# A two-pass prompt attention: the turning of the log-sums put later, the first pass started further ahead, the first loads reordered

## The chip, the core and the metric

The kernel runs on one core of one Trainium2 chip. The metric is device time in microseconds of one execution. The kernel is one decoding step of a small decoder (one convolution layer, then one attention layer) for a prompt of 1024 tokens and for eight samples of one token each.

## What is computed

The change lies in the attention of the prompt. Cut to that, the reference is:

```python
# q, k, v: (1024 tokens, 16 heads, 64); C = cumsum of the log forget gates, per head
def fox_attend(q, k, v, C):              # swept in blocks of 128 queries
    s = einsum('bqhd,bkhd->bhqk', q, k) / sqrt(64)
    s = s + C[query] - C[key]
    s = where(key <= query, s, -inf)
    p = softmax(s, axis=-1)
    return einsum('bhqk,bkhd->bqhd', p, v)
# layer output: x + (o * silu(z)) @ w_out
```

Ahead of it stand a gated convolution layer and the projections to q, k, v and z, behind it the output projection. All of these, and the attention of the eight samples over their paged caches, are untouched by the change.

## The kernel before

The program runs through stages: the convolution layer, the projections (with the samples' attention worked in beside them), the prompt attention, and the output projection. In the profiled execution the prompt attention begins at about 980 us and ends at about 1312 us of a span of 1442.5 us.

**Two passes.** Products are made to nearly full precision from a high and a low part of each operand, so a product takes two or three matmuls. The attention of a head is done in two passes over the scores.

- The *first pass*, `first(h, ...)`, goes through the eight query blocks of 128 in the order `QORD` = 0, 4, 1, 5, 2, 6, 3, 7. For block i, TensorE writes the scores against (i+1)*128 keys to PSUM (L1162, L1163, and L1165 for the mask), VectorE takes the negative maximum (`nm`, L1166), and ScalarE takes exp with that bias and sums it (L1168). Below, F5.7 is block 7 of head 5; a head's first pass is eight such items.
- After blocks 3 and 7, `logsum` (L1178 to L1182) makes for four blocks at once the maximum plus the logarithm of the sum: one small ScalarE instruction, then three small VectorE instructions of 128x4 elements. Its inner function `turn` (L1186 to L1190) lets TensorE transpose the result (`lt`), ScalarE copy it out of PSUM, and SyncE send it by two small DMAs to two rows of the head's query tile `q2`. Below, T5.0 and T5.1 are the two turns of head 5.
- The *second pass*, `second(h, ...)`, makes the scores again, transposed (`st`, L1225, L1226), with the rows that `turn` wrote standing in the product, so that exp gives the softmax itself. It goes through two halves c of 512 queries and, in each, pairs of key blocks: six items a head. Below, S5.12 is head 5, half 1, key blocks 2 and 3. ScalarE takes the exp to `pt` (L1235), GpSimd (POOL in the profile) rounds it to `ph` (L198), GpSimd or VectorE takes the rest `pl` (L1239), and TensorE weighs the values with both (`weigh`, L1205, L1206, into `po`). At a half's end ScalarE copies one part out (`tb`, L1209) and VectorE adds (`og`, L1210); after an odd head VectorE and ScalarE gate and split the pair of heads (L1252, `oh` L1254, `ol` L1255).

**PSUM.** The large score tiles of both passes (F of blocks 4 to 7, S items 00, 10, 12 and 14) share one pool of two buffers (`psS`); the small ones and the turns share one of three (`psQ`); the weighed values have a single buffer (`psO`). So a large item starts when the exp of the one two before it in that pool is done, and the weighing of a half starts when `og` of the half before is done.

**What sets the order.** `firsts()` and `seconds()` yield an item at a time. `LEAD` first-pass items are written out ahead, then the two are taken in turn by the pattern `PAT` = FSFSFSFFSFSFFS, eight F and six S to a head. Steps that should come later are put off by `put_off(n, f)`, which runs f once more than n items have gone by: exp by `DEXP` = 1, `logsum` by `DEXP + DLS` = 1 item, `turn` by `DLT` items after its `logsum`. What is written out in this order is then ordered once more when the program is built: a scheduler lists each engine's instructions by the order written and by its own estimate of when each can start. Every engine then runs its list strictly in order.

**Loads.** A head's tiles are fetched by `load_qk(h)` (eight DMAs, six of them of 256 KB) and `load_rest(h)` (the values `vh` of 512 KB, and `sz` of 512 KB for each pair of heads), all issued by SyncE, which also issues the small DMAs of `turn`. A DMA there waits until the one eight before it has landed. Heads 0 and 1 are loaded before the stage; head 2's tiles and head 0's values are the stage's first loads. From then on `seconds()` loads values one head and query and key tiles three heads ahead of the second pass.

Of the kernel before, what the change touches and what calls it, by code (L numbers as in the profile page):

```python
# [99 lines left out]
ST = 2  # L100
FT = 1
VE = 2
LEAD = 13
W0E = 2
THR = 2
CHQ = 1
# [12 lines left out]
START = "w0 n0 t0 w1 n1 n2"  # L119
X0V = 1  # L120
DLS = 0
DLT = 3
PAT = "FSFSFSFFSFSFFS"


def f32(ap):
    return ap.bitcast(F32)
# [7 lines left out]
def tile_step(ctx, tc, xt, st, stT, vecs, cwT, win, wout, wqkv, wf, wbo, hvec, qgf, ck, cv, cf, pt,  # L135
# [16 lines left out]
    def table(name):  # L152
        tc.keep_in_program_order(S.preload_act_table_set(name))
# [478 lines left out]
    def load_qk(h):  # L632
        pool = hd if h % 4 > 1 else h0
        q1, q2, k1, k2 = [pool.tile([P, 1024], F32R, tag=nm, name=nm, bufs=2) for nm in ("q1", "q2", "k1", "k2")]
        fs = slice(h * HD, (h + 1) * HD)

        for out, src in ((q1[0:HD], qt_scr[0, fs]), (k1[0:HD], kt_scr[0, fs]), (q1[HD:P], qt_scr[1, fs]), (k1[HD:P], kt_scr[0, fs]),
                         (q2[0:HD], qt_scr[0, fs]), (k2[0:HD], kt_scr[1, fs]), (q2[HD:HD + 4], c_scr[h, 0:4]), (k2[HD:HD + 6], c_scr[h, 4:10])):
            SY.dma_start(out=f32(out), in_=src)
        return q1, q2, k1, k2  # L640

    def load_rest(h):
        vh = hd.tile([P, 8, P], F32R, tag="vh", name="vh", bufs=VHB)
        SY.dma_start(out=f32(vh), in_=vt_scr[h].rearrange("(i p) f -> p i f", p=P))
        hp, e = divmod(h, 2)
        if e == 0:
            sz = szs[hp] = ld.tile([P, T], F32, tag="sz", name="sz", bufs=1)
            SY.dma_start(out=sz, in_=z_scr[hp])
        return vh

    qk0 = []
# [470 lines left out]
    with pat:  # L1122
# [8 lines left out]
        def qbank(name):  # L1131
            if OBANK:
                return psO.tile([P, 512], F32, tag="o", name=name)
            return psQ.tile([P, 512], F32, tag="q", name=name)
# [7 lines left out]
        def put_off(n, f):  # L1142
            off_.append([n, f])

        def catch_up(n=1):
            for x in list(off_):
                x[0] -= n
                if x[0] < 0:
                    off_.remove(x)
                    x[1]()  # L1150

        def first(h, q1, q2, k1, k2):
            nm = sm.tile([P, 8], F32, tag="nm", name="nm")
            sr = sm.tile([P, 8], F32, tag="sr", name="sr")
            for qi in QORD:
                nk = (qi + 1) * P
                qsl = slice(qi * P, (qi + 1) * P)
                ss = qbank("ss") if nk in SMF else psS.tile([P, 1024], F32, tag="s", name="ss")
                for b0 in range(0, nk, 512):
                    w = min(512, nk - b0)  # L1160
                    lastb = b0 + w == nk
                    PE.matmul(ss[:, b0:b0 + w], q1[:, qsl], k1[:, b0:b0 + w], start=True, stop=False)  # L1162
                    PE.matmul(ss[:, b0:b0 + w], q2[0:HD + 4, qsl], k2[0:HD + 4, b0:b0 + w], start=False, stop=not lastb)  # L1163
                    if lastb:
                        PE.matmul(ss[:, qsl], identb, maskb, start=False, stop=True)  # L1165
                V.tensor_reduce(out=nm[:, qi:qi + 1], in_=ss[:, :nk], axis=AX.X, op=ALU.max, negate=True)  # L1166
                def expsum(ss=ss, nk=nk, qi=qi):
                    S.activation(out=ss[:, :nk], in_=ss[:, :nk], func=AF.Exp, bias=nm[:, qi:qi + 1], accum_out=sr[:, qi:qi + 1])  # L1168

                put_off(DEXP, expsum)  # L1170
                catch_up()
                if qi % 4 == 3:
                    put_off(DEXP + DLS, lambda qi=qi: logsum(h, qi // 4, nm, sr, q2))
                yield nk

        def logsum(h, c, nm, sr, q2):
            cs = slice(c * 4, c * 4 + 4)
            S.activation(out=sr[:, cs], in_=sr[:, cs], func=AF.Ln)  # L1178
            V.tensor_tensor(out=nm[:, cs], in0=nm[:, cs], in1=sr[:, cs], op=ALU.subtract)
            lc = sm.tile([P, 8], F32R, tag="lc", name="lc")  # L1180
            V.tensor_copy(out=lc[:, 0:4], in_=nm[:, cs])
            V.tensor_tensor(out=lc[:, 4:8], in0=nm[:, cs], in1=f32(lc[:, 0:4]), op=ALU.subtract)  # L1182

            def turn():
                ps = qbank("lt")
                PE.transpose(f32r(ps[0:8, 0:P]), lc, identr)  # L1186
                lt = sm.tile([8, P], F32, tag="lt", name="lt")
                S.copy(out=lt, in_=ps[0:8, 0:P])
                for a in range(2):
                    SY.dma_start(out=f32(q2[HD + 4 + a:HD + 5 + a, c * 512:(c + 1) * 512]).rearrange("a (t q) -> a t q", t=4), in_=lt[4 * a:4 * a + 4])  # L1190

            put_off(DLT, turn)

# [60 lines left out]
                    S.copy(out=oa.hi(hp, a, b - a), in_=og[:, a:b])  # L1254
                    V.tensor_tensor(out=oa.lo(hp, a, b - a), in0=og[:, a:b], in1=f32(oa.hi(hp, a, b - a)), op=ALU.subtract)  # L1255

        hs = qk0 + [load_qk(2)]
        vhs = [load_rest(0)]
        table("natural_log_exp_and_others")
        oa = Act("o")  # L1260

        def firsts():
            for h in range(NH):
                yield from first(h, *hs[h])

        def seconds():
            for h in range(NH):
                if h + 1 < NH:
                    vhs.append(load_rest(h + 1))
                if h + 3 < NH:  # L1270
                    hs.append(load_qk(h + 3))
                yield from second(h, *hs[h], vhs[h])


        if MAN:
            pat.enter_context(tc.manual_schedule(engines={getattr(mybir.EngineType, e) for e in MAN.split()}))
        fs_, ss_, n = firsts(), seconds(), 0
        for _ in range(LEAD):
            next(fs_)
        while True:  # L1280
            x = next(fs_, None) if PAT[n % len(PAT)] == "F" else None
# [6 lines left out]
    with ExitStack() as po_:  # L1288
# [16 lines left out]
        def resid(hf, t0, tn):  # L1305
            x = wk.tile([P, 512], F32, tag="xr", name="xr", bufs=10)
            SY.dma_start(out=x[:tn], in_=x1_scr[t0:t0 + tn, hf * 512:(hf + 1) * 512])
            return x
# [44 lines left out]
        for t in range(8):  # L1353
# [7 lines left out]
            x = resid(1, t * P, P)  # L1361
# [56 lines left out]
```

## Time and profile before

| | us |
|---|---|
| median of 3 runs (lowest, highest) | 1446.85 (1446.19, 1448.22) |
| the profiled execution, its own time | 1444.18 |
| its span, first to last instruction | 1442.5 |
| prompt attention within the span | about 980 to 1312 |
| TensorE busy over the span | 1266.6 (88%) |
| VectorE busy over the span | 1151.2 (80%) |
| GpSimd busy over the span | 800.8 (56%) |
| ScalarE busy over the span | 732.2 (51%) |

The shares are means over stages with different limits; the change touches only the attention stage, so that stage is read by itself: by stretches, by the waits in it, and instruction by instruction in one pair of heads (the pattern of work repeats every two heads, since which engine makes `pl` differs between even and odd heads). In the rows, PE is TensorE, PEld its weight loads, DVE VectorE, ACT ScalarE, POOL GpSimd and SP SyncE. A wait in brackets behind an instruction is the time its engine stood idle before it and what released it.

### The profile page before, as it was taken

What the parts mean: (1) busy time and instruction counts of PE and PEld (TensorE: products, weight loads), DVE (VectorE), ACT (ScalarE), POOL (GpSimd) and SP (SyncE); (2) the same over time, 40 slices, a digit from 0 to 9 for tenths busy, and PEclk for the clock granted to TensorE, in tenths of its full rate; (3) what the DMA queues carried; (4) which work ended last, traced back from release to release, by engine and by line L of the source; (5) the groups of instructions that cost most, each with busy time, mean ns of one, the idle gap of its engine ahead of it and who ended that gap; (6) DMA issues with size and microseconds to landing.
All of it is one profiled execution on the core that took longest, in us unless ns stands there. A gap on an engine that the chain in (4) does not pass through costs nothing. (4 is left out here: it accounts for less than half of the span.)

```text
span 1442.5 us, 21436 instructions
## 1 busy us (share of the span) xinstructions
PE 1266.6 (88%) x6543; PEld 1050.8 (73%) x6543; DVE 1151.2 (80%) x1844; ACT 732.2 (51%) x1922; POOL 800.8 (56%) x603
## 2 busy tenths in 40 slices
PE   5999999988999799987997979796988888885988
PEld 4999999987778587765776768695766666664866
DVE  6999999998844489999899989873688787876851
ACT  6666554755745666765662223114666665662100
POOL 4598895982220063447466555750666565666940
PEclk9999999998999899999998989898899998998989
DMA  5111010111244666788788888888455555413841
GB/s 209 57 59 59 31 30 20 45 44 62 81 146 125 177 184 209 232 229 260 242 266 274 275 269 267 248 210 186 106 123 122 114 134 120 90 45 109 280 159 38
DMA packets 155531, 213.95 MB, mean 148 GB/s; under 512 B 14058, under 2 KB 82282, under 8 KB 155400
## 3 DMA queue, kind: packets, MB, share of 16 engines
q1 hardware_dynamic: 137879, 202.09, 48.1%
q10 hardware_dynamic: 16896, 8.39, 2.0%
q0 software_dynamic: 640, 2.10, 0.5%
q8 instruction: 52, 0.85, 0.3%
q14 instruction: 64, 0.52, 0.1%
HBM read 165.22 MB, written 48.13 MB: 148 GB/s over the span
## 5 line engine op out<-in xcount | busy, mean ns | idle before, releaser
L347 POOL TENSOR_TENSOR cvt<-cvt 128x512 f32<-128x512 f32 (+4 forms) x179 | 242.0, 1388 | 44.5 <-ACT cvt L343 41.7
L906 POOL TENSOR_TENSOR kh<-kh,qb 128x512 f32<-128x512 f32 x96 | 137.4, 1446 | 131.4 <-DMA kh<-in_ck 87.9
L352 DVE SCALAR_TENSOR_TENSOR acc<-u,cw,acc 128x512 f32<-128x512 f32 (+4 forms) x285 | 195.8, 742 | 0.1
L198 POOL TENSOR_SCALAR ph<-pt 128x896 fp32r<-128x896 f32 (+1 forms) x96 | 90.7, 960 | 153.3 <-ACT pt L1235 139.7
L685 POOL TENSOR_TENSOR av<-av,vt 128x512 f32<-128x512 f32 x80 | 134.2, 1698 | 71.0 <-DVE vt L683 64.2
L1105 PE MATMUL pq<-wp,acth 128*128 128x512 f32 x384 | 158.4, 412 | 0.0
L1107 PE MATMUL pq<-wp,actl 128*128 128x512 f32 x384 | 155.2, 404 | 0.0
L1106 PE MATMUL pq<-wp,acth 128*128 128x512 f32 x384 | 154.8, 403 | 0.0
L1166 DVE TENSOR_REDUCE nm<-ss 128x1 f32<-128x128 f32 (+7 forms) x128 | 93.3, 750 | 75.5 <-PE ss L1165 62.7
L683 DVE TENSOR_TENSOR vt<-vt,lg 128x512 f32<-128x512 f32 x112 | 127.8, 1173 | 13.4 <-DMA vt<-in_cv 13.2
L343 ACT ACTIVATE cvt<-u,cw 128x512 f32<-128x512 f32 (+4 forms) x195 | 125.7, 717 | 16.2 <-DVE wl L271 8.3
L1168 ACT ACTIVATE ss<-ss,nm 128x128 f32<-128x128 f32 (+7 forms) x128 | 91.1, 712 | 68.6 <-DVE nm L1166 68.3
L1239 POOL TENSOR_TENSOR pl<-pt,ph 128x384 fp32r<-128x384 f32 (+2 forms) x56 | 103.5, 1854 | 2.3
L1162 PE MATMUL ss<-k,q 128*128 128x512 f32 (+2 forms) x192 | 78.9, 411 | 13.6 <-ACT ss L1168 12.6
L1235 ACT ACTIVATE pt<-st 128x896 f32<-128x896 f32 (+1 forms) x96 | 75.5, 805 | 30.1 <-PE st L1233 19.4
L1107 PEld LDWEIGHTS pq<-wp,actl 128*128 128x128 f32 x384 | 74.3, 193 | 18.7 <-issue 0.8
L1105 PEld LDWEIGHTS pq<-wp,acth 128*128 128x128 f32 x384 | 74.7, 195 | 17.8 <-ACT hsq L826 1.0
L1106 PEld LDWEIGHTS pq<-wp,acth 128*128 128x128 f32 x384 | 74.7, 194 | 16.7 <-issue 0.5
L907 DVE TENSOR_REDUCE lg<-kh 128x8 f32<-128x512 f32 x128 | 82.7, 673 | 4.6 <-POOL kh L906 4.5
L1205 PE MATMUL po<-ph,vh 128*128 128x512 f32 x192 | 72.4, 382 | 7.8 <-DVE og L1210 4.5
L1226 PE MATMUL st<-q,k 70*128 70x512 f32 (+1 forms) x192 | 67.1, 367 | 9.8 <-DMA q<-lt 9.8
L1225 PE MATMUL st<-q,k 128*128 128x512 f32 (+1 forms) x192 | 72.4, 384 | 2.3 <-ACT pt L1235 2.1
(337 smaller groups left out, 3777.5 us busy)
## 6 DMA issues: line engine op xcount, KB each, us to landing
kh<-in_ck SPq DMA_DIRECT2D x128, 256.0 KB
vt<-in_cv SPq DMA_DIRECT2D x128, 256.0 KB
wraw<-in_wqkv SPq DMA_DIRECT2D x56, 256.0 KB
wr<-in_win SPq DMA_DIRECT2D x24, 512.0 KB
q<-qt_scr SPq DMA_DIRECT2D x48, 256.0 KB
k<-kt_scr SPq DMA_DIRECT2D x48, 256.0 KB
vt_scr<-vx SPq DMA_DIRECT2D x32, 256.0 KB
vh<-vt_scr SPq DMA_DIRECT2D x16, 512.0 KB
```

What stands on the lines that cost most here:

```text
L343: S.activation(out=t[:, :m], in_=u[:, lo + j:hi + j], func=AF.Copy, scale=cw[:, c, j:j + 1])
L347: G.tensor_tensor(out=pacc[:, :m], in0=pacc[:, :m], in1=t[:, :m], op=ALU.add)
L352: V.scalar_tensor_tensor(out=acc, in0=u[:, lo + jd:hi + jd], scalar=cw[:, c, jd:jd + 1], in1=acc, op0=ALU.mult, op1=ALU.add)
L683: V.tensor_tensor(out=heads(vt[x] if g else ax), in0=heads(vt[x]), in1=over_d(lg[:, p0:p0 + 8], P, 8), op=ALU.mult)
L685: (V if g % VDVE == 3 else G).tensor_tensor(out=ax, in0=ax, in1=vt[x], op=ALU.add)
L906: (V if g % 4 == 3 else G).tensor_tensor(out=kt, in0=kt, in1=qb, op=ALU.mult)
L1105: PE.matmul(ps, na.hi(k, t * P, P), ws[k][:, 0:512], start=(k == 0), stop=False)
L1106: PE.matmul(ps, na.hi(k, t * P, P), ws[k][:, 512:1024], start=False, stop=False)
L1107: PE.matmul(ps, na.lo(k, t * P, P), ws[k][:, 0:512], start=False, stop=(k == KT - 1))
L1166: V.tensor_reduce(out=nm[:, qi:qi + 1], in_=ss[:, :nk], axis=AX.X, op=ALU.max, negate=True)
L1168: S.activation(out=ss[:, :nk], in_=ss[:, :nk], func=AF.Exp, bias=nm[:, qi:qi + 1], accum_out=sr[:, qi:qi + 1])
L1239: (G if plo else V).tensor_tensor(out=pl[:, :off], in0=pt_[:, :off], in1=f32(ph[:, :off]), op=ALU.subtract)
```

## The change

Three things are changed. `DLT` goes from 3 to 6, so `turn` is written six items behind its `logsum` in place of three. `LEAD` goes from 13 to 16, so exactly two heads' first passes are written ahead of the second pass. And the stage's first loads are written into the first pass: head 0's values and gate (`load_rest(0)`) after the first item, head 2's query and key tiles (`load_qk(2)`) after the third, where both stood ahead of the stage before, in the other order.

```diff
-LEAD = 13
+LEAD = 16
...
-DLT = 3
+DLT = 6
...
-        hs = qk0 + [load_qk(2)]
-        vhs = [load_rest(0)]
+        hs = list(qk0)
+        vhs = []
         table("natural_log_exp_and_others")
         oa = Act("o")
 
         def firsts():
             for h in range(NH):
-                yield from first(h, *hs[h])
+                for i, x in enumerate(first(h, *hs[h])):
+                    yield x
+
+                    if h == 0 and i == 0:
+                        vhs.append(load_rest(0))
+                    if h == 0 and i == 2:
+                        hs.append(load_qk(2))
```

No instruction is added or taken away. What moves is the place of each instruction in its engine's list, in the attention stage only. Three places follow, as the two built programs have them.

VectorE, the log-sum of head 5's second half. Before: the maximum of F5.7 (`ss_12623`), then F6.1, the gating of a pair of heads, F6.4 (`ss_12661`), a split `ol`, and the three log-sum instructions (L1179, L1181, L1182) that T5.1 waits for.

```order
L1166 TENSOR_REDUCE nm_12443<-ss_12623 128x1
L1166 TENSOR_REDUCE nm_12648<-ss_12690 128x1
L1252 TENSOR_TENSOR og_12186<-og_12186,sz_11968 128x512
L1166 TENSOR_REDUCE nm_12648<-ss_12661 128x1
L1255 TENSOR_TENSOR ol_11642<-og_12186,oh_11641 128x512
L1179 TENSOR_TENSOR nm_12443<-nm_12443,sr_12444 128x4
L1181 CAST lc_12657<-nm_12443 128x4
L1182 TENSOR_TENSOR lc_12657<-nm_12443,lc_12657 128x4
```

VectorE at the same log-sum in the changed program, where F5.7 is `ss_12545` and F6.4 is `ss_12649`:

```order
L1166 TENSOR_REDUCE nm_12374<-ss_12545 128x1
L1255 TENSOR_TENSOR ol_11626<-og_12230,oh_11625 128x512
L1239 TENSOR_TENSOR pl_12561<-pt_12559,ph_12560 128x384
L1166 TENSOR_REDUCE nm_12574<-ss_12649 128x1
L1179 TENSOR_TENSOR nm_12374<-nm_12374,sr_12375 128x4
L1181 CAST lc_12583<-nm_12374 128x4
L1182 TENSOR_TENSOR lc_12583<-nm_12374,lc_12583 128x4
```

The split `ol` now stands ahead of F6.4's maximum, so the log-sum follows that maximum directly. On TensorE, 19 rows stand between F6.4 and T5.1 before (S4.12, some weighing, S4.14), and 11 now (some weighing, S4.10).

ScalarE, around the exp of S5.12 (`pt_12874<-st_12869`). Before, it follows the exp of F7.1 and stands ahead of those of F7.2 (`ss_12930`), F7.5 (`ss_12922`) and F7.3 (`ss_13010`); the two other `pt` are S5.14 and S5.16.

```order
L1168 ACTIVATE ss_12890,sr_12849<-ss_12890,nm_12848 128x256
L1235 ACTIVATE pt_12874<-st_12869 128x1024
L1188 COPY lt_12910<-lt_12908 8x128
L1235 ACTIVATE pt_12903<-st_12896 128x896
L1254 CAST oh_11641<-og_12591 128x512
L1235 ACTIVATE pt_12942<-st_12936 128x384
L1168 ACTIVATE ss_12930,sr_12849<-ss_12930,nm_12848 128x384
L1168 ACTIVATE ss_12922,sr_12849<-ss_12922,nm_12848 128x768
L1168 ACTIVATE ss_13010,sr_12849<-ss_13010,nm_12848 128x512
```

ScalarE at the same place in the changed program: the copy of T6.1, the exps of S5.02 and S5.10, of F7.5, F7.1, F7.2 and F7.3, and then that of S5.12 (`pt_12906<-st_12901`).

```order
L1188 COPY lt_12801<-lt_12799 8x128
L1235 ACTIVATE pt_12863<-st_12857 128x384
L1235 ACTIVATE pt_12881<-st_12876 128x1024
L1168 ACTIVATE ss_12887,sr_12780<-ss_12887,nm_12779 128x768
L1168 ACTIVATE ss_12869,sr_12780<-ss_12869,nm_12779 128x256
L1168 ACTIVATE ss_12895,sr_12780<-ss_12895,nm_12779 128x384
L1168 ACTIVATE ss_12944,sr_12780<-ss_12944,nm_12779 128x512
L1235 ACTIVATE pt_12906<-st_12901 128x1024
```

The exp of S5.12 now comes behind four of the first pass. S5.14 takes its PSUM buffer.

SyncE, at the start of the stage. Before, head 2's eight loads come first; their last two, then head 0's `vh` and `sz`, head 1's `vh` and the first load of head 3:

```order
L639 DMA q2_11625<-c_scr_76 4x1024
L639 DMA k2_11627<-c_scr_76 6x1024
L644 DMA vh_11636<-vt_scr_73 128x8x128
L648 DMA sz_11638<-z_scr_72 128x1024
L644 DMA vh_11766<-vt_scr_73 128x8x128
L639 DMA q1_11768<-qt_scr_74 64x1024
```

SyncE at the start in the changed program, from the last but one store of the stage before:

```order
L1059 DMA z_scr_72<-zt_11567 128x256
L644 DMA vh_11634<-vt_scr_73 128x8x128
L1059 DMA z_scr_72<-zt_11595 128x256
L648 DMA sz_11636<-z_scr_72 128x1024
L639 DMA q1_11652<-qt_scr_74 64x1024
L639 DMA k1_11654<-kt_scr_75 64x1024
```

Head 0's `vh` and `sz` now stand ahead of head 2's eight loads. Head 1's `vh` and head 3's eight loads follow in both programs, and only behind all of these comes the first small DMA of T0.0.

## Rows read from the trace of the kernel before

**Rows 1.** The page: busy us, share of the span and instructions of each engine.

```profile
PE 1266.6 (88%) x6543; PEld 1050.8 (73%) x6543; DVE 1151.2 (80%) x1844; ACT 732.2 (51%) x1922; POOL 800.8 (56%) x603
```

**Rows 2.** Stretches: length; busy PE, PEld, DVE, ACT, POOL; clock, DMA share, GB/s.

```profile
980.00:1006.00 26.00, 14.04 (x79) 10.47 (x79) 12.59 (x26) 13.61 (x40) 0.00 (x0) 0.83 0.89 196
...
1093.90:1131.80 37.90, 31.83 (x177) 24.18 (x177) 31.05 (x42) 25.86 (x58) 24.90 (x20) 1.00 0.57 128
1131.80:1172.80 41.00, 35.02 (x177) 26.55 (x178) 31.69 (x42) 25.97 (x58) 23.88 (x20) 0.92 0.53 118
...
1212.20:1254.60 42.40, 36.43 (x176) 27.70 (x176) 31.02 (x42) 25.99 (x58) 23.80 (x20) 0.88 0.51 114
...
1286.00:1312.00 26.00, 17.03 (x83) 12.61 (x82) 16.40 (x15) 12.94 (x21) 25.49 (x19) 0.92 0.08 25
```

**Rows 3.** TensorE's waits, 960 to 1310 us: in total, times, longest.

```profile
PE lt L1186 <- DVE lc L1182: 24.0, 20, 2.4
PE ss L1162 <- ACT ss L1168: 12.6, 15, 1.1
PE st L1226 <- DMA q<-lt: 9.8, 2, 9.4
...
PE po L1205 <- DVE og L1210: 0.5, 1, 0.5
```

**Rows 4.** Timeline of TensorE, five turns (T5.1, T6.0 to T7.1): start, us, wait.

```profile
1093.91 0.22 PE L1186 MATMUL lt<-identr,lc 128*8 128x128 f32 x1 [2.36 <-DVE lc L1182]
...
1107.62 0.22 PE L1186 MATMUL lt<-identr,lc 128*8 128x128 f32 x1
1110.04 0.22 PE L1186 MATMUL lt<-identr,lc 128*8 128x128 f32 x1 [0.84 <-DVE lc L1182]
1120.69 0.22 PE L1186 MATMUL lt<-identr,lc 128*8 128x128 f32 x1 [0.55 <-DVE lc L1182]
1131.80 0.22 PE L1186 MATMUL lt<-identr,lc 128*8 128x128 f32 x1 [2.36 <-DVE lc L1182]
```

**Rows 5.** Timeline of POOL and DVE: a log-sum's last step, twice.

```profile
1091.50 2.34 POOL L1239 TENSOR_TENSOR pl<-pt,ph 128x1024 fp32r<-128x1024 f32 x1
1091.66 2.20 DVE L1182 TENSOR_TENSOR lc<-nm,lc 128x4 fp32r<-128x4 f32 x1
...
1120.38 0.16 DVE L1182 TENSOR_TENSOR lc<-nm,lc 128x4 fp32r<-128x4 f32 x1
```

**Rows 6.** Groups by shape, 1093.9 to 1254.6 us: count, busy us, mean ns, idle before.

```profile
L1182 DVE TENSOR_TENSOR lc<-nm,lc 128x4 fp32r<-128x4 f32 x16 | 18.9, 1180 | 0.4
...
L1168 ACT ACTIVATE ss<-ss,nm 128x768 f32<-128x768 f32 x8 | 7.0, 875 | 15.0 <-DVE nm L1166 15.0
...
L1168 ACT ACTIVATE ss<-ss,nm 128x512 f32<-128x512 f32 x8 | 5.3, 657 | 4.5 <-DVE nm L1166 4.5
...
L1168 ACT ACTIVATE ss<-ss,nm 128x384 f32<-128x384 f32 x8 | 4.3, 536 | 3.7 <-DVE nm L1166 3.7
...
L1168 ACT ACTIVATE ss<-ss,nm 128x256 f32<-128x256 f32 x8 | 3.6, 448 | 4.7 <-DVE nm L1166 4.7
```

**Rows 7.** The chain that ended last, in TensorE: start, us, what.

```profile
1095.22 0.23 PE ss L1162
...
1099.25 0.07 PE ss L1165
...
1102.55 0.29 PE po L1206
1102.84 0.18 PE po L1205
```

**Rows 8.** Timeline at the stage's start: SyncE's first load, T0.0, TensorE's long wait.

```profile
980.06 0.45 SPq L639 DMA_DIRECT2D q<-qt_scr  x1
...
989.88 0.25 PE L1186 MATMUL lt<-identr,lc 128*8 128x128 f32 x1
...
1005.13 0.80 PE L1226 MATMUL st<-q,k 70*128 70x512 f32 x1 [9.39 <-DMA q<-lt]
```

## The prediction

> **What bounds the kernel now.** I read the page's busy shares first, then the stretches of the attention stage, then TensorE's waits there, and last single instructions in one pair of heads. Over the whole span TensorE is busy 88% and VectorE 80% [rows 1], but these are means, and the change touches one stage only.
>
> In that stage the pattern repeats every two heads. The last turn of an odd head stands at 1093.91 and at 1131.80 [rows 4]: 37.9 us for a pair while the clock is at its upper level (1.00, which is 2.4 GHz). In that pair TensorE is busy 31.8, VectorE 31.1, ScalarE 25.9, POOL 24.9 [rows 2]. No engine is full; the reader is to see four engines that each run a list in order and wait for one another, TensorE and VectorE with the least to spare. Where a part of a pair falls to the lower level, 1.2 GHz, the pair takes longer: 41.0 us at 0.92 and 42.4 at 0.88 [rows 2]. That the time follows TensorE's clock says that TensorE's list is what paces the stage.
>
> What TensorE does without stops can be counted. It issues 512 columns in 0.235 us, 384 in 0.18, a mask in 0.07 [rows 7]. A head has 9,216 columns in each of first pass, second pass and weighing: 54 times 0.235 is 12.7, and with masks and turns 14.1 us, 28.2 a pair. So 9.7 of the 37.9 us are stops, the refilling after them, and small gaps. The largest stop has a name: TensorE stands at the turn because VectorE hasn't finished `lc`, 24.0 us in 20 times over the stage. Waits for a score buffer (the exp of an earlier block) come second, 12.6 in 15 [rows 3]. In one pair the four turns wait 0, 0.84, 0.55 and 2.36 us [rows 4]: 3.75. The two score-buffer waits of a pair, at the mean of 0.84 [rows 3], add 1.7; what is left is small.
>
> Why is `lc` late? Its last step takes 0.16 us when POOL is idle. At 1091.66 it took 2.20 and ended where POOL's 2.34 us product, begun just before it, ended [rows 5]. Over 16 log-sums the mean is 1.18 [rows 6]. The Trainium skill ("SBUF — State Buffer", section "SBUF: two separate sides") says that a VectorE instruction with two SBUF inputs and a GpSimd one contend for a port pair, which whoever starts first keeps to its end; by that rule, with which the two rows agree, the later turn moves TensorE's place and shortens nothing on VectorE.
>
> **Part 1: the turns, three items later.** No instruction is added, so the price is where each stands. At T5.1 VectorE's list now goes from F6.4's maximum straight to the log-sum, with no split between, but TensorE reaches the turn sooner as well: before, the work between F6.4 and T5.1 was S4.12, 0.94 of weighing and S4.14, 2.8 us by the pace above; now it is 0.94 of weighing and S4.10, 1.9. Against that VectorE needs 0.8 for the maximum and 0.5 for the three small steps, 1.3: no wait if POOL is idle, 1.6 if the last step is held for 2.2 again. At T4.1 the work between is longer than the path, and POOL has nothing ready. At T4.0 and T5.0 the log-sum stands right behind a `pl` that TensorE needs anyway. So the four waits, 3.75 a pair, become between 0 and 1.6; I take 0.6, nearer the free case because only one of the four meets a POOL product in the new list. Gain 3.1 a pair. The small DMAs of the turn move along; they have most of a head's time, about 19 us, until the second pass reads them, so that costs nothing (without that cover each would cost a wait like the 9.39 of [rows 8]).
>
> **Part 2: the lead, and what it sets beside what.** First-pass and second-pass items now meet at another phase. TensorE's list alternates large F and large S items strictly, and the trace of before doesn't show that, so I bound it.
> - The exp of S5.12 now stands behind four first-pass exps: 0.88, 0.45, 0.54 and 0.66 [rows 6], 2.5 us and some 0.8 for reading out the sums. S5.14 needs its buffer; TensorE has 1.9 us of work until then. Wait 0 to 1.4, I take 1.0.
> - F7.4 and F8.4 wait for the exp of block 7 before them, as they do now; F8.4 has less ahead of it. Together 1.7 (as now) to 2.6, I take 2.2.
> - The single buffer of weighed values: W of half 1 waits for `og`, which now stands behind one more exp and one more maximum. Today that is 0.5 us once in the stage [rows 3]. TensorE has 2.0 us of work until then (F6.6, F7.0, S4.14), the path through ScalarE and VectorE takes 1.3 to 3.2; at the odd head another 0 to 0.8. I take 1.6 a pair out of 0 to 2.0.
>
> New and grown waits: 4.8 against today's 1.7, a loss of 3.1 (bounds: 0 and 4.3). On this count the pair stays at 37.9. A second count goes through the pair instruction by instruction with the measured durations, each starting when its engine and its inputs are free: T6.1 comes 19.2 us after T5.1 and T7.1 another 16.8 us later, 36.0, or 1.9 less. It gains because VectorE's maxima, which read PSUM, now stand in a row while POOL does its long products, so that fewer of them collide. That count leaves out small gaps, and for the list of before it runs up to 0.7 us ahead of the trace within a half pair, so it is the low end. I take the middle, 1.0 a pair. Seven pairs: 7.0.
>
> **Part 3: the first loads.** TensorE stands 9.39 us at 1005.13 for the two rows of T0.0, though T0.0 ran at 989.88 [rows 8]: its small DMA is behind head 2's tiles, head 0's and 1's values and head 3's tiles, 4.7 MB, which at 196 GB/s [rows 2] from 980.06 on take until about 1004. All of these still stand ahead of it, so the wait stays, and it hides the reorder: head 2's tiles come 1.0 MB later, 5 us at that rate, and F2.0, which now stands ahead of F1.6, may hold TensorE for 3 to 4 us of the same hole (that wait is free while head 2 lands before about 1002). What the longer lead gives is that F2.1 and F2.2 run in the hole: their exps cost ScalarE 0.45 and 0.54 with reading out, about 1.4 together. Gain 1.5. At the other end nothing changes: over the last two heads POOL is busy 25.5 of 26.0 us [rows 2], with or without the first pass beside it.
>
> **The sum.** 7.0 + 1.5 = 8.5 off the profiled execution's 1444.18 gives 1435.7. The median of the three runs is 2.67 above that execution, so against it: **1438**. Its own range, from half of that to twice: 1430 to 1443.
>
> **Rivals.**
> - *Slower: the new waits outgrow the old.* In Part 2 the three kinds together reach 1.4 a head, 2.6 and 2.0: 7.4 a pair, 5.7 more than today, against 3.1 gained and 1.0 of fewer collisions: 1.6 a pair lost, 11 over the stage, 1456 with the start's gain. It decides once they pass 5.8 a pair. For it: TensorE's stops are already spread over several causes, so taking one away shows the next. Against it: ScalarE has 12 us of slack a pair.
> - *Nothing takes the turn's place.* 24.0 us of waits go [rows 3], and with them the stops ahead of which the clock falls: the pairs at 41.0 and 42.4 would come back to 37.9, which is 7.6 more. With half to three quarters of both, and the start, 17 to 25: about 1425. The Trainium skill ("TensorE: Matmul & The Clock Gate", section "HAM oscillation — how this bites in real kernels") has the clock fall after gaps in TensorE's work; no row of before shows which stop does it.
> - *No change: the log-sum is as late as ever.* POOL holds VectorE at two of four turns still, as in [rows 5] and as the port rule would have it; each costs 1.6, so 3.2 of the 3.75 stays, the buffer waits add 0.5, and with the start's 1.5 it comes to 1445; with one or two us more of buffer waits over the stage, 1444 to 1449. In the scheduler's list the turns did move, so that the change does nothing at all is ruled out.
>
> **How the numbers follow.** About 0.2%, 2.9 us, is what a measurement of this kernel can tell from no change. Forecast (1430 to 1443) 0.38, clean gain (below 1430) 0.14, no change 0.20, slower 0.28. Faster 0.52, same 0.20, slower 0.28. The range leaves out the lower half of the clean gain and the worst third of the slower case, some 0.17 in all: 1425 to 1456.
>
> **What would show it.** Right: TensorE's waits for `lc` fall from 24.0 to below 8; a wait for `og` and more for exps appear, 10 us or more together; the turn-to-turn time of a pair at full clock is 36.0 to 37.7; the wait at the start stays at 7 to 11 us; POOL is full over the last 26 us. Wrong: pairs over 38 us, `lc` still at 15 us or more, or the first second-pass item coming later than 1007.

## The result and the profile after

The changed kernel takes 1426.28 us (median of 4 runs, 1420.24 to 1431.79) against 1446.52 (1440.76 to 1448.22) for the kernel before in the same comparison: a ratio of 0.9889, 95% interval 0.9845 to 0.9933. That is 20 us faster where 8.5 were forecast; it lies in the range given (1425 to 1456), 1.3 us above its lower end, and outside the forecast's own range of 1430 to 1443. Its profiled execution took 1426.27.

The page of the changed kernel, busy us and share of each engine, answers to [rows 1]: VectorE does the same instructions in 11.0 us less (1151.2 before).

```profile
PE 1271.7 (89%) x6543; PEld 1056.1 (74%) x6543; DVE 1140.2 (80%) x1844; ACT 731.1 (51%) x1922; POOL 806.1 (57%) x603
```

Where the 18.2 us of span went, by marks in the two traces: from the first score maximum to the last weighing the attention stage took 333.8 us and takes 316.5, 17.3 less. Ahead of it 4.5 us are gone and behind it 3.6 have come, in stages that the change doesn't touch. Within the stage, from T1.1 to T15.1, seven pairs of heads, it was 277.86 and is 260.06: 17.8 less. The stretches of after answer to [rows 2] (length; busy PE, PEld, DVE, ACT, POOL; clock, DMA share, GB/s): two single pairs at the upper clock level, one pair with a part at the lower, then T15.1 to the last weighing, then all seven pairs.

```profile
1123.55:1158.88 35.33, 31.77 (x176) 24.35 (x177) 28.70 (x42) 25.75 (x58) 24.09 (x19) 1.00 0.63 137
1158.88:1194.26 35.38, 31.76 (x177) 24.37 (x177) 27.94 (x42) 25.65 (x58) 24.45 (x19) 1.00 0.63 138
1085.09:1123.55 38.46, 34.87 (x177) 26.77 (x177) 28.16 (x42) 25.73 (x58) 24.10 (x19) 0.91 0.60 126
1268.40:1293.60 25.20, 20.45 (x84) 16.88 (x85) 17.84 (x13) 9.71 (x15) 22.29 (x16) 0.73 0.11 31
1008.34:1268.40 260.06, 233.69 (x1226) 179.68 (x1227) 194.02 (x281) 178.48 (x398) 168.00 (x133) 0.94 0.53 115
```

The seven pairs of before, the same stretch:

```profile
1014.82:1292.68 277.86, 238.00 (x1235) 180.70 (x1232) 217.05 (x284) 182.19 (x402) 168.33 (x134) 0.94 0.49 111
```

A pair at 1.00 went from 37.9 to 35.35 us; seven times 2.55 is 17.8, as much as the whole difference. The granted clock over the seven pairs is 0.94 in both, so it gave little or nothing. TensorE's busy time in a pair is unchanged (31.8); VectorE's fell from 31.05 to 28.7 and 27.9.

TensorE's waits of after, 955 to 1300 us (in total, times, longest), answer to [rows 3]:

```profile
PE lt L1186 <- DVE lc L1182: 8.2, 8, 1.9
PE po L1206 <- DVE pl L1239: 6.2, 6, 2.3
...
PE po L1205 <- DVE og L1210: 4.7, 10, 1.1
PE po L1205 <- issue: 4.0, 6, 0.7
PE po L1205 <- DVE nm L1179: 3.8, 5, 0.8
PE st L1226 <- DMA q<-lt: 3.4, 1, 3.4
...
PE ss L1163 <- DMA k<-kt_scr: 1.8, 1, 1.8
PE ss L1162 <- DMA k<-kt_scr: 1.7, 1, 1.7
PE st L1225 <- ACT pt L1235: 1.7, 7, 0.4
```

The turns' waits fell from 24.0 to 8.2. The waits of first-pass blocks for a score buffer (`ss`), 12.6 before, are gone; those of second-pass blocks (`st`, 2.1 before) stay at 1.7. In their place stand short waits ahead of the weighing (`po`); "issue" there is a wait for nothing that the profile shows. Of the four turns of a pair, only the last of the odd head still waits (0.84; [rows 4] had 0, 0.84, 0.55, 2.36). The timeline of TensorE below (start, us, wait) has every wait of that pair, the turn's last, and one block without a wait (1153.65); its rows come back further down.

```profile
1132.35 0.47 PE L1205 MATMUL po<-ph,vh 128*128 128x512 f32 x1 [0.76 <-DVE nm L1179]
...
1140.29 0.47 PE L1205 MATMUL po<-ph,vh 128*128 128x512 f32 x1 [0.66 <-issue]
...
1147.80 0.50 PE L1225 MATMUL st<-q,k 128*128 128x512 f32 x1 [0.20 <-ACT pt L1235]
...
1149.22 0.47 PE L1205 MATMUL po<-ph,vh 128*128 128x512 f32 x1 [0.19 <-DVE og L1210]
...
1153.65 0.50 PE L1162 MATMUL ss<-k,q 128*128 128x512 f32 x1
...
1156.50 0.39 PE L1206 MATMUL po<-pl,vh 128*128 128x256 f32 x1 [0.79 <-DVE pl L1239]
...
1158.88 0.22 PE L1186 MATMUL lt<-identr,lc 128*8 128x128 f32 x1 [0.84 <-DVE lc L1182]
```

### The profile page after: what moved, and what is told of

Same layout as the page of the kernel before. It is cut to its first block, busy times and chain, and to the rows that moved or that the text cites. A ratio compares the mean times of both kernels' runs of the same rounds, so it can differ in the third digit from the quotient of the medians.

```text
span 1424.3 us, 21480 instructions
## 1 busy us (share of the span) xinstructions
PE 1271.7 (89%) x6543; PEld 1056.1 (74%) x6543; DVE 1140.2 (80%) x1844; ACT 731.1 (51%) x1922; POOL 806.1 (57%) x603
## 4 chain that ended last, share of the span: by engine, by line
DVE 23%; PE 18%; DMA 7%; issue 6%; POOL 2%; ACT 2%; SPq 1%; DVEq 0%; POOLq 0%; ACTq 0%
DVE vt L683 3%; DVE lg L907 3%; DMA vt<-in_cv 3%; DVE wp L808 2%; PE po L1205 2%; PE ss L1162 2%; PE ss L1163 2%; PE po L1206 2%; PE st L1225 1%; DVE nm L1166 1%; PE st L1226 1%; DVE kh L906 1%; PE py L1318 1%; PE py L1319 1%; PE py L1320 1%
## 5 line engine op out<-in xcount | busy, mean ns | idle before, releaser
L1166 DVE TENSOR_REDUCE nm<-ss 128x1 f32<-128x768 f32 (+7 forms) x128 | 94.1, 752 | 77.7 <-PE ss L1165 76.6
L683 DVE TENSOR_TENSOR vt<-vt,lg 128x512 f32<-128x512 f32 x112 | 132.2, 1215 | 10.9 <-DMA vt<-in_cv 10.7
L343 ACT ACTIVATE cvt<-u,cw 128x512 f32<-128x512 f32 (+4 forms) x195 | 126.1, 719 | 17.3 <-POOL cvt L347 9.4
L1168 ACT ACTIVATE ss<-ss,nm 128x768 f32<-128x768 f32 (+7 forms) x128 | 91.7, 718 | 35.6 <-DVE nm L1166 32.3
L1107 PEld LDWEIGHTS pq<-wp,actl 128*128 128x128 f32 x384 | 74.8, 195 | 18.9 <-issue 0.8
L1206 PE MATMUL po<-pl,vh 128*128 128x512 f32 x192 | 69.5, 381 | 6.8 <-DVE pl L1239 6.2
L1225 PE MATMUL st<-q,k 128*128 128x256 f32 (+2 forms) x192 | 73.5, 389 | 1.7 <-ACT pt L1235 1.7
```

The lines of the kernel that those rows point to most:

```text
L343: S.activation(out=t[:, :m], in_=u[:, lo + j:hi + j], func=AF.Copy, scale=cw[:, c, j:j + 1])
L683: V.tensor_tensor(out=heads(vt[x] if g else ax), in0=heads(vt[x]), in1=over_d(lg[:, p0:p0 + 8], P, 8), op=ALU.mult)
L1107: PE.matmul(ps, na.lo(k, t * P, P), ws[k][:, 0:512], start=False, stop=(k == KT - 1))
```

## Experiments: which of the three edits did it

**Only the lead (16 in place of 13).**

```diff
-LEAD = 13
+LEAD = 16
```

> The kernel before with the first pass 16 items ahead of the second in place of 13, and nothing else: the turns stay three items behind their log-sum, the first loads stay where they were. In the built program VectorE's and TensorE's lists are then almost those of the changed kernel, but the two turns of an odd head stand earlier again. Phase theory (the lead alone sets which maxima, exps and POOL products stand beside each other, and that is where the pair of heads lost 2.5 us): a pair at full clock takes 35.3 to 36.3 us, the waits for a score buffer stay gone (under 3 us over the stage, 12.6 before), and the time is 1426 to 1433. Turn theory (the wait for the log-sum is the whole gain, and the lead only makes room for it): the waits for lc stay at 15 us or more, a pair stays at 37.2 to 38, and the time is 1438 to 1446. Mixed: about 36.5 a pair, 1433 to 1438.

Measured: 1429.51 us, ratio 0.9847 (0.979 to 0.9904). A pair of it at the upper level, by its stretches, and its first two rows of waits:

```profile
1166.65:1202.02 35.37, 31.71 (x177) 24.37 (x177) 28.71 (x42) 25.75 (x58) 24.09 (x19) 1.00 0.62 138
```

```profile
PE lt L1186 <- DVE lc L1182: 9.8, 9, 2.4
PE st L1226 <- DMA q<-lt: 6.8, 1, 6.8
```

That is the changed kernel's pair, to 0.04 us, with the turns still at three items. The phase theory's numbers came: the lead alone gives the pair of the changed kernel and takes the waits for `lc` from 24.0 to 9.8.

**Only the spaced loads** (lead 13, turns at three).

```diff
-        hs = qk0 + [load_qk(2)]
-        vhs = [load_rest(0)]
+        hs = list(qk0)
+        vhs = []
...
+                    if h == 0 and i == 0:
+                        vhs.append(load_rest(0))
+                    if h == 0 and i == 2:
+                        hs.append(load_qk(2))
```

> The kernel before with only the first loads written into the first pass; the lead stays 13, the turns stay at three items. Both theories of the attention's pairs expect 37.9 us a pair at full clock. Theory that the loads do nothing (the same bytes stand ahead of the small DMA of the first turn): from the stage's first load to the first second-pass matmul it takes 24 to 25.5 us as before (25.1), and the time is 1443 to 1448. Theory that the spacing brings the first turn's rows sooner: under 22 us, TensorE's wait there under 5 us (9.39 before), and the time is 1438 to 1443.

Measured: 1447.31 us, ratio 0.9998 (0.9959 to 1.0036); TensorE's wait at the start is 8.80, and a pair at 0.96 takes 39.42, as those of before at 0.96 do (39.41 and 39.42). From the last gate matmul ahead of the stage to the end of that wait it is 23.7 us, where before had 24.7: one microsecond at most, not seen in the time.

**All but the loads** (lead 16, turns at six) and **all but the turns** (lead 16, spaced loads, turns at three).

```diff
-        hs = list(qk0)
-        vhs = []
+        hs = qk0 + [load_qk(2)]
+        vhs = [load_rest(0)]
```

> The changed kernel without the spacing of the first loads (lead 16, turns at six items; loads as before the change). If the loads do nothing, the time is that of the changed kernel within 3 us, 1423 to 1430, and the first stretch from the first load to the first second-pass matmul takes 24 to 25.5 us. If they were what shortened the start, 3 to 6 us come back: 1430 to 1434, with TensorE's waits for DMAs at the stage's start at 9 us or more (6.9 in the changed kernel).

```diff
-DLT = 6
+DLT = 3
```

> The changed kernel with the turns back at three items behind their log-sum; lead 16 and spaced loads stay. Turn theory: the waits for lc come back from 8.2 to 15 us or more, a pair at full clock goes from 35.3 to 37 or more, the time to 1436 or more. Phase theory: VectorE's list differs only in that the log-sum's steps come one maximum sooner, the weighing behind the turn has to wait for og in any case, so the pair is 35.3 to 36.3 and the time within 5 us of the changed kernel, 1422 to 1432.

Measured: 1422.17 us (0.9824, 0.9773 to 0.9875) and 1431.91 (0.989, 0.9835 to 0.9945), with pairs of 35.33 and 35.36 at the upper level, waits for `lc` of 9.0 and 5.8 us, and stages of 312.9 and 314.9 us. All four kernels with lead 16 lie between 312.9 and 316.5, and the intervals of their ratios overlap. Without the spaced loads the wait at the start is one of 9.6 us again and ends 24.3 us behind the last gate matmul, 0.9 later than in the changed kernel; with them and the turns at three it ends at 24.1. The built programs say why the turn's delay does nothing: at lead 16 the lists of TensorE and VectorE are the same from head 8 to head 13, item for item, with turns at three, five, six or seven items. It looks as if the scheduler puts a turn where it expects the log-sum to be ready, and the delay in the source is only a lower bound that this place already passes; the lists alone don't show its reason. A delay of six at lead 13 wasn't tried: the second pass would read rows of head 0 ahead of their being written.

## Experiments: why the lead does it

The rows of [rows 5] suggested that the log-sum is late because POOL's product holds its last step. Two ways to free it were tried.

**The log-sum's operands in PSUM**, at lead 13 and at lead 16:

```diff
+            ps = qbank("lt")
+            ls, ln = ps[:, P:P + 4], ps[:, P + 4:P + 8]
-            S.activation(out=sr[:, cs], in_=sr[:, cs], func=AF.Ln)
-            V.tensor_tensor(out=nm[:, cs], in0=nm[:, cs], in1=sr[:, cs], op=ALU.subtract)
+            S.activation(out=ls, in_=sr[:, cs], func=AF.Ln)
+            V.tensor_tensor(out=ln, in0=nm[:, cs], in1=ls, op=ALU.subtract)
             lc = sm.tile([P, 8], F32R, tag="lc", name="lc")
-            V.tensor_copy(out=lc[:, 0:4], in_=nm[:, cs])
-            V.tensor_tensor(out=lc[:, 4:8], in0=nm[:, cs], in1=f32(lc[:, 0:4]), op=ALU.subtract)
+            V.tensor_copy(out=lc[:, 0:4], in_=ln)
+            V.tensor_tensor(out=lc[:, 4:8], in0=ln, in1=f32(lc[:, 0:4]), op=ALU.subtract)
...
             def turn():
-                ps = qbank("lt")
```

> The kernel before (lead 13, turns at three items, loads as they were), but the three small log-sum steps on VectorE take one operand from PSUM: the logarithm and the difference are put into free columns of the turn's own PSUM tile, so that no step of the log-sum reads two operands from SBUF. Results are the same. The scheduler's list shifts a little with it. Collision theory (the log-sum was late because POOL held it, and that is what a pair of the kernel before pays): the last log-sum step takes 0.16 to 0.3 us everywhere (1.18 in the mean before), TensorE's waits for lc fall from 24.0 to under 8 us, a pair at full clock takes 35.8 to 36.6 us, the time is 1430 to 1438. Order theory (the pair's length comes from where maxima, exps and POOL products stand; the held step only shows up where TensorE stands anyway): the waits for lc fall as well, others take their place, the pair stays at 37.2 us or more, the time at 1440 to 1447.

> Lead 16 with the log-sum's operands in PSUM as in the run above; turns at three items, loads as before the change. Collision theory: the four log-sums of a pair, 0.52 us each for the last step in the changed kernel and up to 1.3 for the first, fall to 0.16 to 0.3, the last 0.84 us wait of a pair for lc goes: pair at full clock 34.3 to 35.2 us, time 1415 to 1424. Rival: a turn's small PSUM buffer, one of three, is now held from the log-sum on, and small score blocks wait for it, or the new list is simply another one: pair 35.6 us or more, time 1425 to 1435.

Measured: 1409.76 us (0.9703, 0.9652 to 0.9755) at lead 13 and 1392.04 (0.961, 0.9558 to 0.9661) at lead 16, both below what either theory said. The groups by shape (count, busy us, mean ns): the last log-sum step in the kernel before, in the changed one, and with PSUM operands at lead 16, where it is L1184.

```profile
L1182 DVE TENSOR_TENSOR lc<-nm,lc 128x4 fp32r<-128x4 f32 x32 | 32.5, 1015 | 0.9
```

```profile
L1182 DVE TENSOR_TENSOR lc<-nm,lc 128x4 fp32r<-128x4 f32 x32 | 15.9, 498 | 0.8
```

```profile
L1184 DVE TENSOR_TENSOR lc<-lt,lc 128x4 fp32r<-128x4 f32 x32 | 5.0, 155 | 0.6
```

So in the changed kernel the step takes half as long in the mean as before, and with an operand in PSUM it is never held (0.16 us at the longest). At lead 16 with PSUM operands TensorE waits for `lc` not once in the stage, and a pair takes 32.34 us with VectorE busy 25.4. Two pairs of it, as stretches:

```profile
1075.28:1107.61 32.33, 30.83 (x179) 24.43 (x178) 25.37 (x42) 25.52 (x59) 25.60 (x20) 1.00 0.69 150
1107.61:1139.95 32.34, 30.84 (x179) 24.45 (x178) 25.40 (x42) 25.55 (x59) 25.66 (x20) 1.00 0.70 150
```

**One step exchanged, the list unchanged.** PSUM operands also shift the scheduler's list. The last run takes that doubt away, in the kernel before:

```diff
-            V.tensor_tensor(out=lc[:, 4:8], in0=nm[:, cs], in1=f32(lc[:, 0:4]), op=ALU.subtract)
+            V.tensor_reduce(out=lc[:, 4:8], in_=f32(lc[:, 0:4]).unsqueeze(2), axis=AX.X, op=ALU.max)
```

> The kernel before, lead 13, with one instruction exchanged: the last log-sum step on VectorE (128x4, high part subtracted from the sum) becomes a reduction over a single element, which reads one operand from SBUF in place of two. What it leaves out: the low part of the log-sum, in whose place the high part stands a second time, so the output differs. Every engine's list in the attention stage is, item for item, that of the kernel before: only the hold can differ. Hold theory (POOL's products hold this one two-operand step, and that costs a pair of the kernel before most of what lead and PSUM operands won): the step takes 0.15 to 0.3 us everywhere, the wait of 2.36 us in a pair falls to 0.3, that of 0.84 to 0, the pair at full clock from 37.9 to 35.0 to 36.2 us, the time to 1422 to 1434. List theory (another step is next, and the pair is set by the list): the waits for lc fall, score-buffer waits grow by as much, the pair stays at 37.2 us or more, the time at 1439 or more. If a one-operand step is held just as well, nothing changes: 1444.

Measured: 1413.89 us, ratio 0.9772 (0.9736 to 0.9809). A pair at the upper level takes 34.6 us, equal to the 34.66 of the PSUM operands at lead 13; pair and time both lie below the lower ends of the hold theory. Timelines of POOL and VectorE in it (start, us), to be set beside [rows 5]: POOL begins its product at 1118.14, the log-sum's last step begins behind it and takes 0.16.

```profile
1118.14 2.38 POOL L1239 TENSOR_TENSOR pl<-pt,ph 128x1024 fp32r<-128x1024 f32 x1
```

```profile
1118.10 0.17 DVE L1181 CAST lc<-nm 128x4 fp32r<-128x4 f32 x1
1118.31 0.16 DVE L1182 TENSOR_REDUCE lc<-lc 128x4 fp32r<-128x4 f32 x1
```

With the same order of work, that one 128x4 step, which stood four times in a pair and took 4.7 us there (18.9 in four pairs, [rows 6]), cost the kernel before 3.3 us a pair; the waits for `lc` fell from 24.0 to 4.7, and the score-buffer waits stayed (12.2). Beside this operation only values differ: the low part, and with it the second pass and the output, which is far off. The second pass's exps take as long as before (4.04 us for the four of 128x1024 in a pair, 4.06 before). So the hold's price in a pair of the kernel before is shown. The whole stage fell by more, 333.8 to 302.1 us, than seven times 3.3: over the seven pairs the granted clock was 0.98 in place of 0.94 as well.

**Other leads** (turns at three items, loads as before), and lead 17 with PSUM operands.

```diff
-LEAD = 13
+LEAD = 17
```

and 18 and 15 in the same line:

> The kernel before with a lead of 17 in place of 13 and nothing else. Cover theory (a longer lead gives every exp and maximum more time before it is needed): at least as good as lead 16, a pair at full clock 34.5 to 35.4 us, the time 1420 to 1430. Phase theory (each lead gives another steady list, and 16 happens to put the maxima in a row beside POOL's products; more lead is no help in itself): the pair differs from 35.35 by 0.7 us or more, most likely upwards, 36 to 38, and the time is 1430 to 1446.

> The kernel before with a lead of 18 and nothing else. Cover theory: 34.5 to 35.4 us a pair at full clock, 1420 to 1430. Phase theory: another value than at 16 and at 17, 35.5 to 38 us a pair, 1428 to 1446; the time then follows no order of 13, 16, 17, 18.

> The kernel before with a lead of 15 and nothing else. With 13 at 37.9, 16 at 35.4, 17 at 34.2 and 18 at about 38 us a pair, a smooth rise of cover up to 17 would put 15 between 35.4 and 36.7 us a pair and 1429 to 1437. If each lead's list is a draw of its own, it may be anywhere from 34 to 38.5, and the waits for lc decide: at 20 us or more over the stage the time is 1438 to 1450, at 10 or less 1410 to 1430.

The PSUM operands of the diff above, put into the kernel with lead 17 and into the whole changed kernel:

> Lead 17 with the log-sum's operands in PSUM; turns at three items, loads as before the change. Additive theory (lead and log-sum are two separate gains: at leads 13 and 16 the PSUM operands took 3.2 and 3.0 us off a pair): lead 17's 34.2 us a pair falls to 31.0 to 32.0, the time to 1378 to 1392, below lead 16 with PSUM operands (1392). Rival (each edit gives a new list, and the sum of two good edits is no better than the best list found; at 32.3 us a pair TensorE is busy 30.8 and has little to give): pair 32.3 us or more, time 1390 to 1410.

> The changed kernel whole (lead 16, turns at six items, spaced loads) with the log-sum's operands in PSUM. If turns and loads do nothing, as without the PSUM operands, the pairs are those of lead 16 with PSUM operands, 32.3 us, the waits for lc are zero, and the time is 1387 to 1397. If the later turns hold the small PSUM buffers too long, waits for them appear and the pair is 33 us or more, 1397 to 1410.

Measured, with the kernels from above beside them (waits of TensorE and the stage from the profiled execution of each). Each ratio is against the kernel before as timed beside that run, where its median was 1444.0 to 1446.5 us, so ratios compare better than times:

| lead, log-sum's operands | time, us | ratio (95%) | waits for `lc`, us | pair at 1.00, us | stage, us |
|---|---|---|---|---|---|
| 13, SBUF (before) | 1446.52 | 1 | 24.0 | 37.89 | 333.8 |
| 15, SBUF | 1431.69 | 0.9928 (0.9881 to 0.9974) | 13.1 | 36.42 | 320.2 |
| 16, SBUF (only the lead) | 1429.51 | 0.9847 (0.979 to 0.9904) | 9.8 | 35.37 | 314.8 |
| 17, SBUF | 1407.01 | 0.97 (0.9652 to 0.9748) | 7.2 | 34.22 | 297.7 |
| 18, SBUF | 1438.83 | 0.9958 (0.9914 to 1.0003) | 28.4 | none (37.97 at 0.96) | 325.0 |
| 13, PSUM | 1409.76 | 0.9703 (0.9652 to 0.9755) | 9.0 | 34.66 | 305.8 |
| 16, PSUM | 1392.04 | 0.961 (0.9558 to 0.9661) | 0 | 32.34 | 280.3 |
| 17, PSUM | 1408.71 | 0.9761 (0.9686 to 0.9836) | 0.5 | 33.63 | 289.7 |
| 16, PSUM, with the turns and loads of the change | 1400.65 | 0.9698 (0.9611 to 0.9785) | 0 | 32.35 | 286.2 |

The cover theory's order holds up to 17, where pair and time lie below the ranges of both theories, and fails at 18. The phase theory's mark came at 17 as well, a pair 0.7 us or more away from 35.35, but downwards, and 18 goes by it. At 18 the log-sum's steps meet POOL's again. Timelines of POOL and VectorE at lead 18: a copy with one operand is held this time, until POOL's product ends.

```profile
1187.68 2.39 POOL L1239 TENSOR_TENSOR pl<-pt,ph 128x1024 fp32r<-128x1024 f32 x1
```

```profile
1187.86 2.23 DVE L1181 CAST lc<-nm 128x4 fp32r<-128x4 f32 x1
1190.13 0.96 DVE L1182 TENSOR_TENSOR lc<-nm,lc 128x4 fp32r<-128x4 f32 x1
```

The additive theory fails at 17: there the PSUM operands take 0.6 us off a pair, not 3, and the ratios, 0.97 and 0.9761, don't tell the two apart. Against lead 16 with PSUM operands it has the longer pair, 33.63 against 32.34, and from the last gate matmul to the first second-pass matmul it took 19.6 us at a clock of 0.73, where lead 16 took 13.9 at 1.00. The last run says once more that the turns and loads of the change bring nothing to a pair: 32.35 with them, 32.34 without. Its time lies above the 1387 to 1397 foreseen: the stage is 5.9 us longer than without them, 2.8 of it in the seven pairs (the first took 35.25 against 32.83), the rest ahead of and behind them. The intervals of the two ratios overlap, so that a loss isn't shown either. Lead 16 with PSUM operands beats both kernels.

What stays open is how the lead itself gains. With the log-sum's operands in PSUM, lead 16 is still 2.3 us a pair better than 13 (32.34 against 34.66); with them in SBUF it was 2.5 (35.37 against 37.89). The lead gains almost as much without the hold on the log-sum as with it, so that the shorter waits for `lc` can't be the whole of its gain. In both cases VectorE's busy time in a pair falls with the lead, by 2.3 (31.0 to 28.7) and by 3.0 (28.4 to 25.4). With PSUM operands most of the second fall is in the split `ol`, as the groups by shape of one pair have it, first at lead 13, then at lead 16:

```profile
L1255 DVE TENSOR_TENSOR ol<-og,oh 128x512 fp32r<-128x512 f32 x2 | 3.5, 1772 | 0.0
```

```profile
L1255 DVE TENSOR_TENSOR ol<-og,oh 128x512 fp32r<-128x512 f32 x2 | 1.4, 680 | 0.0
```

So other steps of VectorE with two operands in SBUF are held less as well. At lead 13 with PSUM operands the turns of a pair still wait 1.9 us and the weighing 2.1; at lead 16 the turns not at all, the weighing 0.5 and the score buffers 1.0. How much of the 2.3 is the hold of other steps and how much the order itself, no run here tells.

## Why the prediction was right, and where its steps failed

**The number.** That the time lies inside the stated range is in part luck. The forecast, 8.5 us of gain, was less than half of what came; the range reached down to 1425 only because it took in the upper half of a rival with a chance of 0.14. Of the signs named for a right prediction, the waits for `lc` came to 8.2 (below 8), a pair to 35.35 (36.0 to 37.7), the waits at the start to 6.95 (7 to 11), those for `og` and for exps to 4.7 and 1.7 (10 or more together, with more for exps), and POOL was busy 23.1 of the last 26 us (full). Each was missed, the first and the third narrowly.

**The bound held in the main.** VectorE's lateness was TensorE's largest stop, and POOL's hold was rightly named as its cause: in the run with the lists unchanged that hold is worth 3.3 us a pair. That TensorE's list alone paces the stage isn't shown. At leads 13 and 16 a pair at 1.00 follows VectorE's busy time: 37.9 with 31.0 before, 35.3 with 28.7 after, 34.7 with 28.4 and 32.3 with 25.4 with PSUM operands, while TensorE's goes only from 31.8 to 30.8. Lead 17 fits this less well, 34.2 with 29.1.

**Part 1 had the size and the wrong edit.** It gave the turns 3.75 to 0.6 us a pair, and they went to 0.84, at the very turn named for it (T5.1's kind). It is the log-sum's first step that is held there, 1.32 us, until POOL's product of 2.28 ends; VectorE's and POOL's timelines of after:

```profile
1157.11 1.32 DVE L1179 TENSOR_TENSOR nm<-nm,sr 128x4 f32<-128x4 f32 x1
```

```profile
1156.13 2.28 POOL L1239 TENSOR_TENSOR pl<-pt,ph 128x896 fp32r<-128x896 f32 x1
```

The upper bound of 1.6 counts the last step twice, free and held; 1.4 is what its terms give. But the later turn did none of it: with the turns at three items a pair takes 35.36 us, with six 35.33. The step that failed is the one that read the change of the turn's place as the work of `DLT`. It compared two programs that differ in three edits; a third, with the lead alone changed, would have shown the same list before any run.

**Part 2 had the new waits far too large.** It set "New and grown waits: 4.8 against today's 1.7, a loss of 3.1". In the pair of after shown above the waits of [rows 3]'s kinds are:

| | before | forecast | after |
|---|---|---|---|
| turns | 3.75 | 0.6 | 0.84 |
| behind exps (score buffers, `pt`) | 2.0 | 3.2 | 0.2 |
| ahead of the weighing (`po`) | 0.2 | 1.6 | 2.4 |

Together 5.95 before and 3.44 after: 2.5 of the 2.55 by which the pair fell. The two lower rows together grew by 0.4, not by 3.1; those ahead of the weighing grew, by more than foreseen. The miss is the middle row, which was to grow and all but went. S5.14's kind did come behind the exp of S5.12's kind, as foreseen, but at 1147.80 it waited 0.20, not 1.0. And F8.4's kind, priced with F7.4's at 2.2, waits for nothing: it starts at 1153.65, while the exp of block 7, which it was to wait for, runs from 1153.49 to 1154.57. The exp that has just ended, at 1153.60, is that of the second-pass item right ahead of it, as ScalarE's timeline of after has it:

```profile
1152.68 0.92 ACT L1235 ACTIVATE pt<-st 128x896 f32<-128x896 f32 x1 [1.04 <-PE st L1233]
1153.49 1.08 ACT L1168 ACTIVATE ss<-ss,nm 128x1024 f32<-128x1024 f32 x1
```

So the bound had the wrong block as its predecessor in the buffer: in the changed program a large item doesn't always take the buffer of the one two before it, as was said of the pool. The count, 37.9, and the walk through the list, 36.0, lay 1.9 apart; the walk, which had fewer collisions in it and was taken as the low end, was 0.65 above the truth, and the middle between the two was not the likeliest value. Seven pairs were to bring 7.0 and brought 17.8.

**The hold by POOL.** The last step took 1.02 us in the mean of all 32 before and 0.50 in after; with one operand from PSUM or as a reduction it took 0.16. The prediction said that the later turn shortens nothing on VectorE, which is so: VectorE is busy 28.7 us in a pair with turns at three and at six. It didn't follow that the lead, which moves VectorE's steps against POOL's, changes how long they are held. Its "no change" rival, POOL holding two of four turns still, fell: one of four waits, 0.84. The Trainium skill ("SBUF — State Buffer", section "Who interferes with whom") has a VectorE instruction with two SBUF inputs contend with a GpSimd instruction that reads SBUF, says that a copy or a cast can contend, and that a reduction on trn2 never does. The traces agree on all three: 2.20 us in [rows 5], 2.23 for the cast at lead 18, and 0.16 for the reduction.

**Part 3 was right on the start.** The wait for T0.0's rows ended 23.4 us behind the last gate matmul (24.7 before). The stage's start was 2.0 us shorter by the marks up to T1.1 (1.5 forecast; 1.3 with the lead alone, none with the loads alone), and F2.0 did stand in the hole, 1.8 and 1.7 us for head 2's tiles beside 3.4 for the rows: 6.95 of waits, just under the 7 to 11 foreseen. These rows are of after, to be set beside [rows 8]:

```profile
988.17 0.30 PE L1162 MATMUL ss<-k,q 128*128 128x128 f32 x1 [1.70 <-DMA k<-kt_scr]
990.30 0.44 PE L1163 MATMUL ss<-k,q 68*128 68x128 f32 x1 [1.83 <-DMA k<-kt_scr]
...
999.84 0.58 PE L1226 MATMUL st<-q,k 70*128 70x256 f32 x1 [3.42 <-DMA q<-lt]
```

The tail was said to stay and grew: T15.1 to the last weighing took 22.7 us and takes 25.2, with POOL busy 22.3 of them (19.4 before) and the clock at 0.73 (0.85 before). The other three kernels with lead 16 and operands in SBUF have 24.4 to 25.4, so it goes with the lead; why, no run tells.

**The rivals.** "Slower" didn't come: the waits ahead of the weighing grew by 2.2 a pair, those behind exps all but went. The "clean gain" had the right time, 1425, by half a wrong reason: its clock term was zero, 0.94 before and after. At lead 16 with PSUM operands, and no wait for `lc` left, six pairs in a row ran at 1.00, as it described. But so did six at lead 17 with 7.2 us of these waits: which stops bring the lower level isn't shown.

## What to carry to other kernels

Where a short VectorE step sits ahead of TensorE and beside long GpSimd work, look at its longest time against its shortest (2.2 and 0.16 us here), and free it at the source: one operand in PSUM, or an operation that the hold doesn't touch. An edit of phase moves the meeting points and may undo itself one step further (lead 17 and lead 18). When a change sets several constants and a scheduler orders the work, build each one alone and compare the lists before pricing any of them.

## What had not been expected of the hardware

A copy of 128x4 elements with a single SBUF operand, 0.17 us otherwise, took 2.23 us at lead 18 and ended with the POOL product begun just before it. And one held step of 128x4 elements was worth 2.3% of the whole kernel: 1413.89 against 1446.78 us, with every list in the stage the same but for that operation, and with the higher clock that came with it.
